# Bias tiles read from 128 stored copies of each bias row instead of squares turned by matrix products, in a two-block kernel on one core

## The chip, the cores and the metric

The kernel runs on one core of a Trainium2 chip. The metric is the time of one execution on the device in microseconds (us), taken as the median of several runs. All arithmetic is in float32; the large matrix products split every operand into a high and a low part and add three products of the fp32r type.

## What is computed

Two transformer blocks follow each other, each of two layers, on 256 tokens of width 1024. The first has a mixer, cross attention to a memory and a gated feed-forward part in each layer; the second has a feed-forward part, a mixer of three attentions and another feed-forward part. What the change touches is the bias that two of the three attentions of the second block add to their scores: a table of 32 buckets by 12 heads, looked up by the distance from query to key.

```
def t5_bucket(dist):
    max_exact = NUM_BUCKETS // 2
    d = jnp.maximum(dist, 0)
...
s_w = (jnp.einsum('bgrqd,bgkd->bgrqk', qb, kb).astype(jnp.float32) * scale
       + head_bias[:, :, t5_bucket(dist_w)])
...
s = (jnp.einsum('bgrqd,bgkd->bgrqk', qb, kb).astype(jnp.float32) * scale
     + head_bias[:, :, t5_bucket(dist)])
```

The bias of one head depends on the distance alone, so a row of 383 numbers holds all that 128 queries and 256 keys need; the tile of 128 by 256 that a score product takes has that row shifted by one element from each query to the next.

## The kernel before, in words

All operations go through a recorder (class `Pace`, whose wrapper is line 151), so every instruction of the trace stands under L151 and has to be told apart by the names of its tiles. The recorder also keeps a rough clock of its own while the program is written. Small pieces of work (attention heads, bias tables) are generators in a list `sides`; `pump` (line 343) writes the next step of a generator between two matrix products when the rough clock says that its inputs are there, and `finish` (line 373) forces out what is left of one. That clock thus sets the order in which instructions stand on each engine. On the chip each engine goes through its instructions in that order.

Weights come in 1 MB loads on SP's queue into three buffers `raw`, are split into `whi` on ScalarE (ACT) and `wlo` on VectorE (DVE), and are multiplied on TensorE (PE) into `acc`.

The function `cross` (line 1251) is the cross attention. It first makes the four blocks of queries (`stat_block`, products `acc` with a moving operand of 256 columns). Each head is then a side generator: products `aux<-mk,cqT` (scores), the row maximum `ngm` on DVE, exponentials `cpr` on ACT, division on DVE, transposes `aux<-ident,cpr` on PE, copy `cpt` on ACT, products `o<-cpt,mv`. After the last block come `finish(bias)` and `out_rows`, the output projection (products `acc` with 512 columns).

The bias of the second block is prepared in the two cross attentions of the first, as one more side generator:

- In layer 0, `bias_rows` (line 1358). Two small products `aux<-c,rb` make 12 rows of 383 (`u`, 12 partitions) and 8 rows of 480 (`uc`). SP stores `u` to `ud` in memory and `uc` to `ucd`, then loads from `ucd` two tiles `uk` with a shift of one element per partition; DVE adds `cmask` to columns of each `uk` (15 operations `bc`), and the result goes to `bcmp`. There is one buffer `uk`.
- In layer 1, `bias_squares` (line 1389). For each pair of heads SP loads `hk` from `ud`, with partition p starting at element p; these rows are in the reverse order. PE multiplies with `anti`, an identity with its columns reversed, ACT copies the product to `bts`, and SP stores that to `btiles`, two squares of 128 by 256 at a time. There are six pairs.

In the mixer of the second block `load_bias` (line 1470) loads one square per head from `btiles` on ACT's queue, 20 in each layer, into four buffers `bt`.

Of the kernel before, what the change touches and what calls it, by code (L numbers as in the profile page):

```python
# [8 lines left out]
F32 = mybir.dt.float32  # L9
# [9 lines left out]
DEPTH, D, S, P = 2, 1024, 256, 128  # L19
# [253 lines left out]
def tile_two_blocks(ctx, tc, I, out):  # L273
# [5 lines left out]
    def nm(s):  # L279
        count[0] += 1  # L280
        return f"{s}_{count[0]}"
# [20 lines left out]
    def aux():  # L302
        t = ps_aux.tile([P, 512], F32, tag="aux", name=nm("aux"))
        auxs.append(t.tensor.name)
        return t
# [20 lines left out]
    def mm(ps, a, b, start, stop, beside=False):  # L326

        nc.beside = beside
        nc.tensor.matmul(ps, a, b, start=start, stop=stop)
        nc.beside = False  # L330
# [4 lines left out]
    def side(gen):  # L335
        sides.append([gen, nc.end, False])
# [36 lines left out]
    def finish(gen):  # L373
        while any(i[0] is gen for i in sides):
            pump(force=True)
# [271 lines left out]
    def const(pool, name, dt=F32, tag=None):  # L647
        lo_, hi_ = C128[name]
        t = pool.tile([P, hi_ - lo_], F32, tag=f"c_{name}", name=nm(name), bufs=1)
        nc.sync.dma_start(t, cst[:, lo_:hi_])  # L650
        return t
# [599 lines left out]
    def cross(l, norm, next_maker):  # L1251
        T = norm.T
        with nc.pool(tc, name=nm("cross"), bufs=2) as mp:

            def load_kv(h):
                out_ = []
                for kind in ("k", "v"):
                    t = mp.tile([P, 2, S], F32, tag=f"m{kind}", name=nm(f"m{kind}"))
                    nc.scalar.dma_start(t.rearrange("p b n -> p (b n)"), kvd[l, kind][h])
                    out_.append(t)  # L1260
                return out_

            kv = {h: load_kv(h) for h in (0, 1)}
            heads = {}
            bias = (bias_rows, bias_squares)[l](mp)
            side(bias)
            O = split_T()

            def head(h, qT):
                yield True  # L1270
                kT, v = kv.pop(h)
                ps = aux()
                for t in (0, 1):
                    for c in (0, 1):
                        mm(ps[:, t * S : (t + 1) * S], qT[:, c, t * P : (t + 1) * P], kT[:, c, :], start=c == 0, stop=c == 1)
                ngm, sums = sm(2, "ngm"), sm(2, "csum")
                nc.vector.tensor_reduce(ngm, ps.rearrange("p (t k) -> p t k", t=2), axis=AX.X, op=ALU.max, negate=True)
                for t in (0, 1):
                    nc.vector.tensor_scalar(ngm[:, t : t + 1], ngm[:, t : t + 1], norm.r[t], None, op0=ALU.mult)
                pr = mp.tile([P, 2, S], F32, tag="cpr", name=nm("cpr"))  # L1280
                for t in (0, 1):
                    nc.scalar.activation(pr[:, t, :], ps[:, t * S : (t + 1) * S], AF.Exp, bias=ngm[:, t : t + 1], scale=norm.r[t], accum_out=sums[:, t : t + 1])
                ri = sm(2, "cri")
                nc.vector.reciprocal(ri, sums)
                for t in (0, 1):
                    nc.vector.tensor_scalar(pr[:, t, :], pr[:, t, :], ri[:, t : t + 1], None, op0=ALU.mult)
                yield True
                ps = aux()
                for t in (0, 1):
                    for c in (0, 1):  # L1290
                        turn(ps[:, c * S + t * P : c * S + (t + 1) * P], pr[:, t, c * P : (c + 1) * P], ident)
                pt = mp.tile([P, 2, S], F32, tag="cpt", name=nm("cpt"))
                nc.scalar.copy(pt.rearrange("p c q -> p (c q)"), ps)
                yield True
                ob = obank(f"o{h % 2}")
                yield from until(nc.free[ob.tensor.name])
                for d in (0, 1):
                    for c in (0, 1):
                        mm(ob[:, d * S : (d + 1) * S], v[:, c, d * P : (d + 1) * P], pt[:, c, :], start=c == 0, stop=c == 1)
                ov = ob.rearrange("p (d q) -> p d q", d=2)  # L1300
                put(O.hi[:, 2 * h : 2 * h + 2, :], O.lo[:, 2 * h : 2 * h + 2, :], ov)
                for kt in (2 * h, 2 * h + 1):
                    O.ready.add((kt, 0))
                    O.ready.add((kt, 1))
                if h < 2:
                    kv[h + 2] = load_kv(h + 2)

            def q_done(h):
                def f(a):
                    if h >= 2:  # L1310
                        finish(heads[h - 2])
                    qT = mp.tile([P, 2, S], F32, tag="cqT", name=nm("cqT"))
                    nc.scalar.activation(qT.rearrange("p c q -> p (c q)"), a[:, :512], AF.Copy, scale=1.0 / 16)
                    heads[h] = head(h, qT)
                    side(heads[h])
                return f

            for h in range(4):
                stat_block(T, 2, 2, q_done(h))
            chain = next_maker()  # L1320
            finish(bias)
            out_rows(lambda k: (O, 0), 8, 4 if units["ffn", l] else 5, chain, units["ffn", l])
        return chain.next

# [25 lines left out]
            nc.scalar.activation(dst.rearrange("p t f -> p (t f)"), a, AF.Sin)  # L1350


    btiles = dpool.tile([12, P, S], F32, tag="btiles", name="btiles")
    bcmp = dpool.tile([P, 240], F32, tag="bcmp", name="bcmp")
    ud = dpool.tile([12, 384], F32, tag="ud", name="ud")
    ucd = dpool.tile([8, 480], F32, tag="ucd", name="ucd")

    def bias_rows(bp):

        one = lambda shape, tag: bp.tile(shape, F32, tag=tag, name=nm(tag), bufs=1)  # L1360
        c32, rb, um, u = one([32, 863], "c32"), one([32, 12], "rb"), one([12, 383], "um"), one([12, 384], "u")
        for t, s_ in ((c32, c32d), (rb, I["rel_bias_2"]), (um, I["umask"])):
            nc.sync.dma_start(t, s_)
        cmask = const(bp, "cmask")
        nc.gpsimd.memset(u[:, 383:], 0.0)
        yield nc.products + 12.0
        ps = aux()
        mm(ps[:12, :383], rb, c32[:, :383], start=True, stop=True)
        nc.vector.tensor_tensor(u[:, :383], ps[:12, :383], um, op=ALU.add)
        nc.sync.dma_start(ud, u)  # L1370
        yield
        ps = aux()
        mm(ps[:8, :480], rb[:, :8], c32[:, 383:863], start=True, stop=True)
        uc = one([8, 480], "uc")
        nc.vector.tensor_copy(uc, ps[:8, :480])
        nc.sync.dma_start(ucd, uc)
        bc = one([P, 2, 4, 2, 15], "bc")
        for t in (0, 1):

            hk = one([P, 8, 225], "uk")  # L1380
            nc.sync.dma_start(hk, bass.AP(tensor=ucd.tensor, offset=ucd.offset + t * P, ap=[[1, P], [480, 8], [1, 225]]))
            yield True
            for n in range(15):
                k = 224 - 16 * n
                nc.vector.tensor_tensor(bc[:, t, :, :, n], hk[:, :, k].rearrange("p (g r) -> p r g", g=2),
                                        cmask[:, t * 15 + n : t * 15 + n + 1].unsqueeze(1).to_broadcast([P, 4, 2]), op=ALU.add)
        nc.sync.dma_start(bcmp, bc.rearrange("p t r g n -> p (t r g n)"))

    def bias_squares(bp):

        anti = const(bp, "anti")
        hks = []

        def load(h):
            hk = bp.tile([P, 2, S], F32, tag="hk", name=nm("hk"))
            nc.sync.dma_start(hk, bass.AP(tensor=ud.tensor, offset=ud.offset + h * 384, ap=[[1, P], [384, 2], [1, S]]))
            hks.append(hk)

        load(0)
        for h in range(0, 12, 2):  # L1400
            if h + 2 < 12:
                load(h + 2)
            yield nc.products + (12.0 if h == 0 else 2.5)
            ps = aux()
            mm(ps, anti, hks.pop(0).rearrange("p h k -> p (h k)"), start=True, stop=True)
            bt = bp.tile([P, 2, S], F32, tag="bts", name=nm("bts"))
            nc.scalar.copy(bt.rearrange("p h k -> p (h k)"), ps)
            nc.sync.dma_start(btiles[h : h + 2].rearrange("h p k -> p h k"), bt)

    def plan_mixer2(l):  # L1410
        w = I["w_in_2"][l]
# [20 lines left out]
    def mixer2(l, T, next_maker):  # L1432
        with nc.pool(tc, name=nm("mix2"), bufs=2) as mp:
# [35 lines left out]

            def load_bias(h):  # L1470
                t = mp.tile([P, S], F32, tag="bt", name=nm("bt"), bufs=4)
                nc.scalar.dma_start(t, btiles[h])
                return t

            def probs(ring, ps, bias, sum_, ngm, first=1e38):
# [598 lines left out]
```

## Time and profile before

| | us |
|---|---|
| median of 3 runs | 2095.59 |
| lowest and highest run | 2090.49, 2095.66 |
| the profiled execution | 2099.48 |
| its span, first to last instruction | 2097.7 |
| PE busy | 2040.0 (97%) |
| DVE busy | 1251.1 (60%) |
| ACT busy | 1096.9 (52%) |

The profiled execution is 3.9 us longer than the median of the runs; 1.8 us of it lie outside its span. Busy time of PE contains time in which its products overlap or run at a lower granted clock. Times in the trace are us from the start of the span.

### The profile page before, as it was taken

The numbers are of one execution on the slowest core, as the hardware profiler recorded it, in microseconds if no ns is written. First come the engines' busy times: TensorE is split into PE (matmuls) and PEld (weight loads), VectorE is DVE, ScalarE is ACT, GpSimd is POOL, SyncE is SP. The second block draws the span as 40 slices with busy tenths as digits, with TensorE's granted clock in tenths as the row PEclk, the third lists the DMA queues.
The fourth block names the chain that finished last, engine by engine and source line by source line (L and its number), as shares of the span: only waits on it lengthen the run. The fifth ranks groups of instructions, "written<-read, shape, count | busy, mean of one in ns | idle before, by whom it ended". The sixth has DMA issues, their size and how long they took to land.

```text
span 2097.7 us, 27293 instructions
## 1 busy us (share of the span) xinstructions
PE 2040.0 (97%) x10446; PEld 1673.8 (80%) x10446; DVE 1251.1 (60%) x2123; ACT 1096.9 (52%) x1842; POOL 92.7 (4%) x112
## 2 busy tenths in 40 slices
PE   7999999999999999999999999999999998999999
PEld 6788888888787788788887677888888886778887
DVE  6766565556763655556466566664565564666553
ACT  5556565445564654555454545654554463546542
POOL 0210000001200000000000000000000000000000
PEclk9999999999999999999999999999999999999999
DMA  7555565645465555465545644555555455555552
GB/s 241 184 191 190 184 203 179 220 160 189 166 212 157 194 183 207 162 201 176 198 142 172 215 135 165 193 180 200 181 181 193 164 186 171 170 151 184 178 199 102
DMA packets 200610, 380.79 MB, mean 182 GB/s; under 512 B 14288, under 2 KB 70400, under 8 KB 200480
## 3 DMA queue, kind: packets, MB, share of 16 engines
q1 hardware_dynamic: 188960, 366.46, 53.0%
q10 hardware_dynamic: 11520, 12.59, 2.0%
q8 instruction: 82, 1.34, 0.2%
q14 instruction: 48, 0.39, 0.1%
HBM read 372.03 MB, written 6.99 MB: 181 GB/s over the span
## 4 chain that ended last, share of the span: by engine, by line
PE 82%; DVE 7%; ACT 4%; DMA 4%; issue 2%; POOL 1%; SPq 0%; ACTq 0%; DVEq 0%; POOLq 0%
PE acc L151 74%; PE aux L151 7%; DVE wlo L151 3%; DMA raw<-in_w_in_dram 2%; PE o L151 2%; ACT whi L151 2%; DMA hk<-ud 1%; ACT thi L151 1%; DVE h L151 0%; ACT cpr L151 0%; DVE rs L151 0%; DVE t L151 0%; DMA mem<-in_mem_dram 0%; DVE ngm L151 0%; DMA nb<-cdram 0%
## 5 line engine op out<-in xcount | busy, mean ns | idle before, releaser
L151 PE MATMUL acc<-whi,thi 128*128 128x512 f32 (+1 forms) x1760 | 704.2, 400 | 6.8 <-ACT kvout L151 2.7
L151 PE MATMUL acc<-whi,tlo 128*128 128x512 f32 (+1 forms) x1760 | 685.0, 389 | 2.7 <-DVE tlo L151 2.6
L151 PE MATMUL acc<-wlo,thi 128*128 128x512 f32 (+1 forms) x1760 | 684.0, 389 | 2.8 <-DVE wlo L151 2.6
L151 DVE TENSOR_TENSOR wlo<-raw,whi 128x1024 fp32r<-128x1024 f32 (+1 forms) x370 | 443.2, 1212 | 293.9 <-ACT whi L151 292.7
L151 ACT CAST whi<-raw 128x1024 fp32r<-128x1024 f32 (+1 forms) x370 | 377.1, 1037 | 259.0 <-PE acc L151 209.3
L151 DVE SCALAR_TENSOR_TENSOR wlo<-raw,prm,whi 128x512 fp32r<-128x512 f32 (+1 forms) x592 | 392.4, 718 | 177.2 <-ACT whi L151 176.9
L151 ACT ACTIVATE whi<-raw,prm 128x512 fp32r<-128x512 f32 (+1 forms) x592 | 371.6, 694 | 93.2 <-PE acc L151 89.7
L151 PEld LDWEIGHTS acc<-whi,thi 128*128 128x128 f32 x1760 | 332.8, 189 | 85.1 <-issue 14.2
L151 PEld LDWEIGHTS acc<-whi,tlo 128*128 128x128 f32 x1760 | 332.1, 189 | 74.9 <-DVE tlo L151 6.7
L151 PEld LDWEIGHTS acc<-wlo,thi 128*128 128x128 f32 x1760 | 333.0, 189 | 66.6 <-DVE wlo L151 6.0
L151 PE MATMUL acc<-whi,ahi 128*128 128x512 f32 x528 | 206.8, 392 | 0.3
L151 PE MATMUL acc<-whi,alo 128*128 128x512 f32 x528 | 205.6, 389 | 0.0
L151 PE MATMUL acc<-wlo,ahi 128*128 128x512 f32 x528 | 205.5, 389 | 0.0
L151 POOL TENSOR_TENSOR r<-v,mhalf 128x1 f32<-128x1 f32 (+3 forms) x46 | 52.2, 1135 | 1538.4 <-DVE v L151 1538.4
L151 DVE SCALAR_TENSOR_TENSOR silu<-acc,r,silu 128x512 f32<-128x512 f32 (+1 forms) x72 | 47.5, 702 | 118.2 <-PE acc L151 94.2
L151 PEld LDWEIGHTS acc<-whi,ahi 128*128 128x128 f32 x528 | 99.1, 188 | 21.6 <-ACT whi L151 1.5
L151 PEld LDWEIGHTS acc<-whi,alo 128*128 128x128 f32 x528 | 99.1, 188 | 20.7
L151 PEld LDWEIGHTS acc<-wlo,ahi 128*128 128x128 f32 x528 | 99.2, 188 | 20.0
L151 PE MATMUL acc<-thi,whi 128*128 128x256 f32 x384 | 113.0, 294 | 0.0
L151 ACT ACTIVATE silu<-acc,r 128x512 f32<-128x512 f32 (+1 forms) x72 | 43.1, 650 | 127.7 <-PE acc L151 127.6
L151 PE MATMUL acc<-tlo,whi 128*128 128x256 f32 x384 | 108.6, 283 | 0.0
L151 PE MATMUL acc<-thi,wlo 128*128 128x256 f32 x384 | 108.5, 283 | 0.0
(299 smaller groups left out, 1815.7 us busy)
## 6 DMA issues: line engine op xcount, KB each, us to landing
raw<-in_w_in_dram SPq DMA_DIRECT2D x65, 1024.0 KB, 5.1
raw<-in_ffn_w_down_dram SPq DMA_DIRECT2D x44, 1024.0 KB, 4.9
raw<-in_ffn_w_gate_dram SPq DMA_DIRECT2D x40, 1024.0 KB, 5.0
raw<-in_ffn_w_up_dram SPq DMA_DIRECT2D x40, 1024.0 KB, 5.0
raw<-in_w_down_dram SPq DMA_DIRECT2D x22, 1024.0 KB, 4.8
raw<-in_w_gate_dram SPq DMA_DIRECT2D x20, 1024.0 KB, 5.0
raw<-in_w_up_dram SPq DMA_DIRECT2D x20, 1024.0 KB, 5.0
raw<-in_w_out_dram SPq DMA_DIRECT2D x16, 1024.0 KB, 5.5
```

The lines of the kernel that those rows point to most:

```text
L151: return f(*args, **kwargs)
```

## The change

The store of 18 KB to `ud` becomes a store of the same 12 rows, each 128 times one after the other, to `urep`: 1536 rows of 384 floats, 2.36 MB. The source is still `u` on 12 partitions, with a step of 0 over the copies. `load_bias` takes a tile from the copies of its head: partition p starts at element 127 + 383 p, so each partition reads 256 floats one element earlier in the row than the one before, which is the order that the reversed identity gave. `bias_squares` is gone, with its six loads, products, copies and stores, its load of `anti` and the memory `btiles`; the cross attention of layer 1 has no bias work.

```
-            bias = (bias_rows, bias_squares)[l](mp)
-            side(bias)
+            bias = bias_rows(mp) if l == 0 else None
+            if bias:
+                side(bias)
...
-            finish(bias)
+            if bias:
+                finish(bias)
             out_rows(lambda k: (O, 0), 8, 4 if units["ffn", l] else 5, chain, units["ffn", l])
...
-    btiles = dpool.tile([12, P, S], F32, tag="btiles", name="btiles")
+    urep = dpool.tile([12, P, 384], F32, tag="urep", name="urep")
...
-        nc.sync.dma_start(ud, u)
+        nc.sync.dma_start(urep, u.unsqueeze(1).to_broadcast([12, P, 384]))
...
-    def bias_squares(bp):
-
-        anti = const(bp, "anti")
...
-            yield nc.products + (12.0 if h == 0 else 2.5)
-            ps = aux()
-            mm(ps, anti, hks.pop(0).rearrange("p h k -> p (h k)"), start=True, stop=True)
-            bt = bp.tile([P, 2, S], F32, tag="bts", name=nm("bts"))
-            nc.scalar.copy(bt.rearrange("p h k -> p (h k)"), ps)
-            nc.sync.dma_start(btiles[h : h + 2].rearrange("h p k -> p h k"), bt)
...
-                nc.scalar.dma_start(t, btiles[h])
+
+                nc.scalar.dma_start(t, bass.AP(tensor=urep.tensor, offset=urep.offset + h * P * 384 + P - 1, ap=[[383, P], [1, S]]))
```

The change also moves instructions, since the recorder's clock counts the bytes of the new store. In the cross attention of layer 0, DVE has these rows around the first operations on `uk`, before the change:

```order
L151 TENSOR_TENSOR wlo_2288<-raw_1987,whi_2287 128x1024
L151 TENSOR_TENSOR bc_2230<-uk_2231,cmask_2068 128x8 x15
L151 TENSOR_TENSOR tlo_1951<-o_2335,thi_1950 128x512
L151 TENSOR_TENSOR wlo_2349<-raw_2087,whi_2348 128x1024
L151 TENSOR_REDUCE ngm_2363<-aux_2358 128x2
```

and with it:

```order
L151 TENSOR_TENSOR wlo_2287<-raw_1986,whi_2286 128x1024
L151 TENSOR_TENSOR tlo_1950<-o_2317,thi_1949 128x512
L151 TENSOR_TENSOR wlo_2331<-raw_2086,whi_2330 128x1024
L151 TENSOR_TENSOR bc_2229<-uk_2230,cmask_2067 128x8 x15
L151 TENSOR_REDUCE ngm_2362<-aux_2357 128x2
```

The 15 additions to the first `uk` now stand straight ahead of the row maximum `ngm` of the last head. On PE, at the same place, the last head's scores are followed before the change by 12 products of the output projection (the first three of them are shown), its transposes, 6 more products and `o`:

```order
L151 MATMUL acc_2245<-tlo_1590,whi_2077 128x256
L151 MATMUL acc_2245<-thi_1589,wlo_2078 128x256
L151 MATMUL aux_2358<-mk_2221,cqT_2352 128x256 x4
L151 MATMUL acc_2391<-whi_2120,thi_1950 128x512
L151 MATMUL acc_2391<-wlo_2121,thi_1950 128x512
L151 MATMUL acc_2391<-whi_2120,tlo_1951 128x512
```

and with it by nothing in between:

```order
L151 MATMUL acc_2244<-thi_1588,wlo_2077 128x256
L151 MATMUL aux_2357<-mk_2220,cqT_2334 128x256 x4
L151 MATMUL aux_2374<-ident_90,cpr_2367 128x128 x4
L151 MATMUL o_2381<-cpt_2379,mv_2222 128x256 x4
L151 MATMUL acc_2404<-whi_2119,thi_1949 128x512
L151 MATMUL acc_2404<-wlo_2120,thi_1949 128x512
```

`finish(bias)` now drives the last head to its end ahead of the output projection, and those 18 products come after `o`. On SP the row `urep<-u` stands where `ud<-u` stood, ahead of `ucd<-uc` and `uk<-ucd`. In the cross attention of layer 1, SP has before the change, from the third and fourth load of output weights on:

```order
L151 DMA raw_5908<-in_w_co_dram 128x2x1024
L151 DMA btiles<-bts_5937 128x2x256
L151 DMA hk_5940<-ud 128x2x256
L151 DMA btiles<-bts_5965 128x2x256
L151 DMA hk_5968<-ud 128x2x256
L151 DMA btiles<-bts_6004 128x2x256
L151 DMA hk_6007<-ud 128x2x256
L151 DMA raw_6025<-in_w_gate_dram 128x4x512
```

and with it:

```order
L151 DMA raw_5805<-in_w_co_dram 128x2x1024
L151 DMA raw_5901<-in_w_co_dram 128x2x1024
L151 DMA raw_5997<-in_w_gate_dram 128x4x512
L151 DMA gain_6043<-in_post_cross_g_dram 128x1024
L151 DMA raw_6082<-in_w_gate_dram 128x4x512
```

All stores to `btiles` and loads of `hk` are gone between the weight loads, and on PE the six products with `hk` are gone while the order of the heads stays interleaved with other products.

## Rows read from the trace of the kernel before

**Rows 1.** The profile page: the chain that ended last, by line.
```profile
PE acc L151 74%; PE aux L151 7%; DVE wlo L151 3%; DMA raw<-in_w_in_dram 2%; PE o L151 2%; ACT whi L151 2%; DMA hk<-ud 1%; ACT thi L151 1%; DVE h L151 0%; ACT cpr L151 0%; DVE rs L151 0%; DVE t L151 0%; DMA mem<-in_mem_dram 0%; DVE ngm L151 0%; DMA nb<-cdram 0%
```
**Rows 2.** Stretches: length, busy PE, PEld, DVE, ACT, POOL; granted clock, DMA share, GB/s.
```profile
614.40:662.70 48.30, 43.81 (x237) 36.01 (x238) 18.25 (x37) 21.17 (x42) 0.00 (x0) 0.96 0.61 198
193.00:234.20 41.20, 39.09 (x229) 32.86 (x230) 21.56 (x69) 17.76 (x37) 0.00 (x0) 1.00 0.59 202
```
**Rows 3.** The chain in order of time, cross attention of layer 1: start, us, what.
```profile
630.75 0.87 PE aux L151 x2
...
645.23 6.16 DMA hk<-ud
```
**Rows 4.** Groups of PE, 614 to 662: busy, mean ns | idle before, releaser.
```profile
L151 PE MATMUL aux<-hk,anti 128*128 128x512 f32 x12 | 6.3, 607 | 3.8 <-DMA hk<-ud 3.8
```
**Rows 5.** Instructions of PE in order: start, us, what [idle before].
```profile
225.41 1.99 PE L151 MATMUL aux<-mk,cqT 128*128 128x256 f32 x8 [1.41 <-ACT cqT L151]
...
651.53 1.10 PE L151 MATMUL aux<-hk,anti 128*128 128x512 f32 x2 [2.59 <-DMA hk<-ud]
652.46 3.47 PE L151 MATMUL aux<-mk,cqT 128*128 128x256 f32 x8
```
**Rows 6.** Stretch after the second wait for hk, columns as in rows 2.
```profile
652.50:656.00 3.50, 3.50 (x10) 2.79 (x9) 0.03 (x1) 0.59 (x1) 0.00 (x0) 0.52 0.25 91
```
**Rows 7.** Groups of PE, 205 to 216, layer 0.
```profile
L151 PE MATMUL aux<-c,rb 32*12 32x383 f32 (+1 forms) x4 | 1.8, 524 | 0.0
```
**Rows 8.** Instructions of SP in order, cross attention of layer 0: start, us of issue.
```profile
209.46 0.37 SPq L151 DMA_DIRECT2D raw<-in_w_co_dram  x1
210.70 0.32 SPq L151 DMA_DIRECT2D ud<-u  x1
213.90 0.29 SPq L151 DMA_DIRECT2D ucd<-uc  x1
215.98 0.38 SPq L151 DMA_DIRECT2D uk<-ucd  x1
221.45 0.40 SPq L151 DMA_DIRECT2D raw<-in_w_ck_dram  x1
222.60 0.36 SPq L151 DMA_DIRECT2D uk<-ucd  x1
```
**Rows 9.** DMA queues (packets, MB, share) and issues (count, KB, median us to landing).
```profile
q1 hardware_dynamic: 188960, 366.46, 53.0%
...
mk<-kvd ACTq DMA_DIRECT2D x8, 256.0 KB, 4.1
...
uk<-ucd SPq DMA_DIRECT2D x2, 900.0 KB, 7.0
hk<-ud SPq DMA_DIRECT2D x6, 256.0 KB, 5.2
...
bcmp<-bc SPq DMA_DIRECT2D x1, 120.0 KB, 1.7
```
**Rows 10.** Instructions of DVE in order, layer 0.
```profile
221.34 1.24 DVE L151 TENSOR_TENSOR bc<-uk,cmask 128x8 f32<-128x8 f32 x15
...
224.89 1.23 DVE L151 TENSOR_TENSOR wlo<-raw,whi 128x1024 fp32r<-128x1024 f32 x1 [0.25 <-ACT whi L151]
227.44 0.69 DVE L151 TENSOR_REDUCE ngm<-aux 128x2 f32<-128x512 f32 x1 [1.32 <-PE aux L151]
```
**Rows 11.** The chain in order of time, last head of layer 0.
```profile
230.32 0.70 PE aux L151 x4
231.03 1.40 PE acc L151 x6
232.42 1.73 PE o L151 x8
```
**Rows 12.** Instructions of ACT in order, the same head.
```profile
231.12 0.59 ACT L151 COPY cpt<-aux 128x512 f32<-128x512 f32 x1 [0.50 <-PE aux L151]
```
**Rows 13.** Tile bt: idle time of DVE before operations on it (us, times).
```profile
  DMA bt<-btiles: 13.1, 5
```

More of the change, by code (lines that the diff above doesn't have):

```diff
@@ L1350, in rotary_tables @@
             nc.scalar.activation(dst.rearrange("p t f -> p (t f)"), a, AF.Sin)
-    btiles = dpool.tile([12, P, S], F32, tag="btiles", name="btiles")
+    urep = dpool.tile([12, P, 384], F32, tag="urep", name="urep")
     bcmp = dpool.tile([P, 240], F32, tag="bcmp", name="bcmp")
-    ud = dpool.tile([12, 384], F32, tag="ud", name="ud")
     ucd = dpool.tile([8, 480], F32, tag="ucd", name="ucd")
@@ L1387, in bias_rows @@
         nc.sync.dma_start(bcmp, bc.rearrange("p t r g n -> p (t r g n)"))
-    def bias_squares(bp):
-        anti = const(bp, "anti")
[L1392 to L1402, printed above, removed]
-            yield nc.products + (12.0 if h == 0 else 2.5)
-            ps = aux()
-            mm(ps, anti, hks.pop(0).rearrange("p h k -> p (h k)"), start=True, stop=True)
-            bt = bp.tile([P, 2, S], F32, tag="bts", name=nm("bts"))
-            nc.scalar.copy(bt.rearrange("p h k -> p (h k)"), ps)
-            nc.sync.dma_start(btiles[h : h + 2].rearrange("h p k -> p h k"), bt)
     def plan_mixer2(l):
```

## The prediction

> **What bounds the kernel now.** I read the chain that ended last first. By line it is products on PE almost throughout, and the only transfer of the bias work in it is `hk<-ud` with 1% [rows 1]. So the kernel is bound by TensorE's work and by the few places where PE waits; a change is worth what it takes off PE there. Next I read the two cross attentions as stretches, each from the first head's scores to the end of the last head's `o`. They hold the same products in the program's order (126 with 256 columns, 18 with 512, four heads), yet layer 1 takes 48.3 us and layer 0 takes 41.2 [rows 2]. The reader should see that the longer one has less work on DVE (18.3 us against 21.6) and a granted clock of 0.96: what makes it long are products and waits of PE. Which waits is shown by PE's own rows and the chain [rows 3 to 6]. Last I read SP, DVE and PE around the bias rows in layer 0 [rows 8 to 12], since the new store stands there.
>
> **The change, part by part.**
>
> *Layer 1 loses the squares.* Six products of `hk` with the reversed identity go; each takes 0.87 us of the chain [rows 3], 5.2 us together. PE waits for `hk` twice, 3.8 us in all, the second time 2.6 us [rows 4, 5]; a load of `hk` took over 6 us there, from issue to release [rows 3]. [...] Sum 10.8 us. The stretches give a check: layer 1 is 7.1 us longer [rows 2], and layer 0 has two things that layer 1 won't have, 1.8 us of small products `c,rb` [rows 7] and a wait of 1.4 us for the last head's `cqT` [rows 5], which six products of the output projection will cover in layer 1: 7.1 + 1.8 + 1.4 = 10.3. I take 10.5 us gained. The six copies on ACT, the loads and stores on SP and the load of `anti` were beside this work and cost nothing of their own; nothing replaces them, and a head's chain stays covered by other products in layer 1. The weight loads behind them on SP come earlier. What is late next there is PE itself.
>
> *Layer 0 loses its cover.* After the last head's scores, PE now has that head's transposes and `o`, and only then the 18 products of the output projection which hid the latency. Those are 3 x 1.40 = 4.2 us of work [rows 11] that now comes after. Between transposes and `o` 0.65 us are won back: the transposes start at 230.32 and `o` at 232.42, but its input `cpt` is there at 231.12 + 0.59 = 231.7, so 1.4 us is enough instead of 2.1 [rows 11, 12]. Cost without any further wait: 3.55 us, plus 1.8 us if the clock falls in the gap of over 4 us that opens between scores and transposes, as it did after 2.6 us of idle in layer 1.
>
> *The store grows from 18 KB to 2.36 MB.* This decides the case. `ucd<-uc` stands behind it on SP's queue, and SP cannot issue the first `uk` before `ucd` has landed. The additions `bc` on that `uk` now stand on DVE right ahead of the last head's `ngm`. So: store late, `ucd` late, `uk` late, DVE blocked, PE idle with no product ahead of the head. Let T be the time that the store's data take.
> - Rates: queue q1 moved 366.46 MB in 53.0% of 16 engines' span of 2097.7 us, 20.6 GB/s for an engine that is busy, 330 for 16 [rows 9]. The store of 120 KB from 128 partitions lands in 1.7 us [rows 9], 0.37 of them data by that rate, so a transfer has 1.33 us beside its data.
> - Start: the weight load ahead is issued at 209.46 [rows 8] and has 1 MB, so its data end at 209.46 + 1.33 + 3.2 = 214.0. The store runs from 214.0 to 214.0 + T.
> - `ucd` lands some 0.7 us later, and `uk` is issued. The row of `uk` says 7.0 us [rows 9], of which a 1 MB load issued just ahead of the second one [rows 8] has 3.2; by rate it is 1.33 + 2.8 = 4.1. I take 4. `uk` is there at 218.7 + T.
> - DVE is free for it at 224.89 + 1.23 = 226.1 [rows 10], so T up to 7.4 us is hidden. Beyond that `bc` takes 1.24 us and `ngm` starts at 219.94 + T, against 227.44 before [rows 10]: T - 7.5 us late.
>
> With the lost cover the cost is T - 7.5 + 3.55 = T - 3.95 us, plus 1.8 for the clock.
>
> How long is T? No row has a large store from few partitions. Low end: all 16 engines at full rate, 2.36 MB / 330 = 7.2 us; if each of the 12 source rows has one engine, 9.6 us. High end: the rate goes with the share of 128 partitions, 12/128 of 330 = 31 GB/s, 76 us. The nearest row is `ucd`: 15 KB from 8 partitions were stored at 213.90 and released the next load at 215.98 [rows 8], 2.08 us, longer than the 1.7 us of the eight times larger store from 128 partitions [rows 9]. If the excess of 0.38 us is all data, 8 partitions give 40 GB/s and 12 give 61, T = 39 us; part of it may be the weight load still ahead, so this is rather too long. I take T = 27 us, the middle in ratio of 9.6 and 76, below the 39 of that row; the other values stay for the range.
>
> [...]
>
> *Reading the tiles.* 40 loads of 128 KB now start their partitions 1532 bytes apart, with 1 KB each as before. `hk` has such 1 KB runs one element apart: 5.2 us against 4.1 for 256 KB of `mk` [rows 9], so at most 0.55 us more for a `bt`, at least nothing. DVE waits five times for a `bt` [rows 13]: 0 to 2.8 us. The loads of `hk` stood between stores and weights, `mk` did not, so I take 0.
>
> *Sum.* -10.5 + (27 - 3.95) + 1.8 = +14.4 us: from the profiled 2099.5 to 2113.9. That execution was 3.9 us above the median of the runs, so for a median I add to 2095.6: **2110 us**. Break even lies at T = 12.7 us.
>
> **The rivals.**
> 1. *The store is quick and mostly covered (not slower).* For it: 12 or 16 engines at the rate that q1 shows. Against it: `ucd`. T = 9.6 gives -10.5 + 5.65 + 1.8 = -3.0, 2092.5 us; T up to 7.4 gives -5.2, 2090.4, and 2088.6 if the clock stays up. It decides below T = 12.7. Between that and T = 19 the cost stays within 0.3% as well.
> 2. *The store takes longer than `ucd`'s rate says.* T = 39 gives 2122, T = 76 gives 2159. For it: partitions are few. Against it: most of `ucd`'s 2.08 us are common to all transfers.
> 3. *The bias tiles come later*, a new wait in the second block: +2.8 us on top, 2113. For it: the five waits; against: 1 KB runs stay 1 KB.
>
> **How the numbers follow.** About 0.3%, 6.3 us, is what a measurement of this kernel can tell from no change. Forecast (T from 19 to 39, rival 3 within it): 0.58. Rival 2 beyond T = 39: 0.09. T from 12.7 to 19: 0.09. Rival 1: 0.24, of which 0.06 for the gain of over 6.3 us that needs a hidden store and a steady clock. So slower 0.67, same 0.27, faster 0.06. The range reaches from the covered store, 2090, to T = 40, 2123; outside it are 0.05 below and 0.09 above. The forecast's own range is 2102 to 2122.
>
> **What would show it.** In layer 1, the stretch from the first scores to the last `o` near 38 us, no wait for `hk` and a clock of 1.00. In layer 0, `ucd` issued early but `uk` only some 28 us later, DVE idle before `bc<-uk`, PE idle for about 24 us before `ident,cpr`, and a low clock after it. The forecast is wrong if SP issues `uk` before about 230, or if PE's gap there is under 10 us; the step at fault is then T. If the gap is there and the time is not, the gain in layer 1 or the loads `bt` were mis-sized.

## The result and the profile after

The changed kernel takes **2117.78 us** (median of 5 runs, 2115.39 to 2119.97) against 2095.66 us for the kernel before in the same measurement: a ratio of 1.0107, 95% interval 1.0094 to 1.0119, so 22.1 us or 1.1% slower. The forecast was 2110 us in a range of 2090 to 2123. The profiled execution of the changed kernel took 2115.39 us, 2.4 us less than its median; the one before stood 3.9 us above its median. So the two traces differ by 15.9 us only, and what the change did is better read from stretches of them than from their ends.

The page's chain by line, the counterpart of [rows 1], has a new transfer in it, and `hk<-ud` is gone:

```profile
PE acc L151 75%; PE aux L151 7%; DVE wlo L151 3%; PE o L151 2%; DMA raw<-in_w_in_dram 2%; DMA ucd<-uc 1%; ACT whi L151 1%; ACT thi L151 0%; DVE h L151 0%; ACT cpr L151 0%; DVE t L151 0%; DVE ngm L151 0%; DVE x L151 0%; DMA uk<-ucd 0%; DVE tlo L151 0%
```

That 1% is the chain's wait for the little store behind the big one. Four views show how. The instructions of SP around the bias rows in layer 0 (start, us of issue), to be held against [rows 8]:

```profile
209.69 0.91 SPq L151 DMA_DIRECT2D urep<-u  x1
212.90 9.37 SPq L151 DMA_DIRECT2D ucd<-uc  x1
243.63 0.38 SPq L151 DMA_DIRECT2D uk<-ucd  x1
...
250.84 0.37 SPq L151 DMA_DIRECT2D uk<-ucd  x1
...
263.22 5.29 SPq L151 DMA_DIRECT2D raw<-in_w_gate_dram  x2
```

The first `uk` is issued at 243.63; before the change it was 215.98. Even to issue `ucd` took SP 9.37 us. DVE and PE at the same place (start, us, what, idle before), to be held against [rows 10 to 12]:

```profile
249.56 1.25 DVE L151 TENSOR_TENSOR bc<-uk,cmask 128x8 f32<-128x8 f32 x15 [24.45 <-DMA uk<-ucd]
250.72 0.69 DVE L151 TENSOR_REDUCE ngm<-aux 128x2 f32<-128x512 f32 x1
```

```profile
224.41 1.99 PE L151 MATMUL aux<-mk,cqT 128*128 128x256 f32 x8 [1.41 <-ACT cqT L151]
253.69 1.09 PE L151 MATMUL aux<-ident,cpr 128*128 128x128 f32 x4 [27.28 <-DVE cpr L151]
255.78 3.78 PE L151 MATMUL o<-cpt,mv 128*128 128x256 f32 x8 [1.01 <-ACT cpt L151]
```

DVE stands for 24.45 us in front of `bc`, with the last head's `ngm` behind it, and PE has no product to do for 27.28 us. The stretches, columns as in [rows 2], tell the rest:

```profile
642.85:698.03 55.18, 53.95 (x296) 45.89 (x297) 26.67 (x49) 25.55 (x51) 0.54 (x1) 1.00 0.43 150
642.80:682.50 39.70, 38.42 (x228) 33.18 (x229) 18.25 (x37) 17.74 (x36) 0.00 (x0) 1.00 0.45 159
191.99:284.79 92.80, 62.58 (x330) 52.36 (x331) 32.71 (x86) 29.01 (x57) 1.65 (x3) 0.83 0.58 148
...
230.20:260.90 30.70, 6.21 (x16) 4.85 (x17) 3.65 (x23) 3.09 (x7) 0.00 (x0) 0.50 0.63 143
```

The second row answers to the 48.30 us of [rows 2]: the cross attention of layer 1 is 8.6 us shorter, at a granted clock of 1.00 instead of 0.96. The third is layer 0 from its first head's scores to the first transposes `aux<-ident,x` behind the output projection, and the first is layer 1 measured in the same way. The same two stretches before the change, layer 0 and then layer 1:

```profile
192.99:254.57 61.58, 59.47 (x331) 50.20 (x332) 32.62 (x86) 28.81 (x57) 1.65 (x3) 1.00 0.54 186
```
```profile
614.40:678.89 64.49, 60.00 (x308) 49.30 (x309) 26.67 (x49) 28.99 (x57) 0.54 (x1) 0.97 0.55 178
```

Layer 0 lost 92.80 - 61.58 = **31.2 us**. Layer 1, between the starts of the same two products, went from 64.47 to 55.17 us and gained **9.3 us**. The difference, 21.9 us, is what the medians show (22.1). From these two stretches the experiments below are read as well; wherever nothing in them was changed they come out the same to 0.4 us in all traces, while executions differ by some us elsewhere.

### The profile page after: what moved, and what is told of

Read it like the earlier page. It is cut to its first block, busy times and chain, and to the rows that moved or that the text cites. A ratio compares the mean times of both kernels' runs of the same rounds, so it can differ in the third digit from the quotient of the medians.

```text
span 2113.6 us, 27236 instructions
## 1 busy us (share of the span) xinstructions
PE 2034.5 (96%) x10434; PEld 1670.8 (79%) x10434; DVE 1251.4 (59%) x2123; ACT 1093.5 (52%) x1836; POOL 92.6 (4%) x112
## 4 chain that ended last, share of the span: by engine, by line
PE 84%; DVE 6%; DMA 4%; ACT 4%; issue 2%; POOL 0%; ACTq 0%; SPq 0%; DVEq 0%
PE acc L151 75%; PE aux L151 7%; DVE wlo L151 3%; PE o L151 2%; DMA raw<-in_w_in_dram 2%; DMA ucd<-uc 1%; ACT whi L151 1%; ACT thi L151 0%; DVE h L151 0%; ACT cpr L151 0%; DVE t L151 0%; DVE ngm L151 0%; DVE x L151 0%; DMA uk<-ucd 0%; DVE tlo L151 0%
```

## Experiments: what makes the store slow

The theory after the result: T, the time of the store's data, is about 30 us because its twelve source rows lie side by side on partitions 0 to 11, and T goes one for one into PE's gap. By the trace's packet records the store's 1536 packets ran from 212.8 to 243.1 us, T = 30.3 us, and one took 213 ns in the median; a packet of `ud`, of the same 1536 bytes, took 65 ns in the run with the small store in the old order (below). Three runs move the rows of `u` to other partitions. The small product that makes the rows gets more columns for it, and ahead of it GpSimd clears two tiles and SP makes one more small load; the rest stays as it is.

```
-        c32, rb, um, u = one([32, 863], "c32"), one([32, 12], "rb"), one([12, 383], "um"), one([12, 384], "u")
+        c32, rb, um, u = one([32, 863], "c32"), one([32, 12], "rb"), one([23, 383], "um"), one([23, 384], "u")
+        rbs = one([32, 23], "rbs")
+        nc.gpsimd.memset(rbs, 0.0)
+        nc.gpsimd.memset(um, 0.0)
-        for t, s_ in ((c32, c32d), (rb, I["rel_bias_2"]), (um, I["umask"])):
+        for t, s_ in ((c32, c32d), (rb, I["rel_bias_2"]), (rbs[:, ::2], I["rel_bias_2"]), (um[::2], I["umask"])):
...
-        mm(ps[:12, :383], rb, c32[:, :383], start=True, stop=True)
+        mm(ps[:23, :383], rbs, c32[:, :383], start=True, stop=True)
...
-        nc.sync.dma_start(urep, u.unsqueeze(1).to_broadcast([12, P, 384]))
+        nc.sync.dma_start(urep, u[::2].unsqueeze(1).to_broadcast([12, P, 384]))
```

**Rows at a distance of 2 partitions.**

> The 12 rows of u lie on partitions 0, 2, 4 to 22 instead of 0 to 11, and the same 1536 packets of 1536 bytes leave from there; the order on every engine is that of the changed kernel. Theory (the store is slow for where its source rows lie: packets from neighbouring partitions stand in each other's way, T = 30.3 us): with twice the distance T halves to about 15 us, uk is issued some 15 us earlier, and the kernel takes 2102 to 2104 us. [...] Rival A (T is set by the number of source rows or of DMA engines that serve them, 12 either way) and rival B (T is set by the writing side in memory): T stays at 30 us and the time at 2117 to 2118 us.

Measured: 2099.55 us, ratio 1.0025 (1.0014 to 1.0036). T = 14.9 us, `uk` issued at 227.67, both as the theory said; the time is 2.5 us below the 2102 to 2104 that it gave.

**Rows at a distance of 9** (the same edit with 100 partitions and `::9`).

> As the run before, with the rows of u on partitions 0, 9, 18 to 99. Theory: T falls further; a quarter of 30.3 is 7.6 us, but 128 packets of a row, one behind the other at the 65 ns that a packet of ud took in the kernel before, are 8.3 us, so T = 8 to 10 us. Then the loss in layer 0 is 31.2 - 21 = 10 us or less, some 5 to 8 us with a shorter clock loss, and the kernel takes 2092 to 2097 us, the time of the kernel before. Rivals A and B: T stays at 30 us, 2117 to 2118 us. A rival C, that the reordering by itself costs most of the loss: T falls, but the time stays above 2105 us.

Measured: 2095.58 us, ratio 1.0004 (0.9994 to 1.0014). T = 9.3 us, `uk` issued at 224.10.

**Rows at a distance of 8** (89 partitions and `::8`).

> As the run with the rows of u on partitions 0, 9 to 99, with a distance of 8 instead of 9: partitions 0, 8 to 88. It tells whether what counts is the distance of neighbouring rows or the group that a partition belongs to. [...] Rival L (only closely neighbouring partitions stand in each other's way): T is 9 to 10 us, the rate 300 GB/s, the time 2094 to 2097 us.

Measured: 2098.35 us, ratio 1.0023 (1.0009 to 1.0038). T = 14.9 us, `uk` issued at 227.70.

The view of all DMA traffic in a stretch inside the store shows the rate: the changed kernel from 228 to 242 us, then the distance of 2 (219 to 226) and of 9 (218 to 223), a fence each. With the distance of 9 a part belongs to another queue (q1 is SP's queue, q10 ACT's; packets, MB, share):

```profile
DMA packets 701, 1.08 MB, mean 77 GB/s; under 512 B 0, under 2 KB 701, under 8 KB 701
```
```profile
DMA packets 708, 1.09 MB, mean 155 GB/s; under 512 B 2, under 2 KB 705, under 8 KB 708
```
```profile
DMA packets 975, 1.51 MB, mean 302 GB/s; under 512 B 11, under 2 KB 921, under 8 KB 975
...
q1 hardware_dynamic: 910, 1.40, 73.9%
q10 hardware_dynamic: 65, 0.11, 5.8%
```

and for the distance of 8 the same view, 40 slices of 214 to 230 us:

```profile
GB/s 346 348 216 200 200 204 207 198 227 212 201 204 211 193 227 207 212 250 228 192 155 108 96 108 104 96 108 104 96 108 97 93 60 0 0 0 20 58 270 295
```

The store alone ran at 77, 154 (1.08 MB in 7 us) and 280 GB/s (1.40 MB in 5 us), and one of its packets took 213, 113 and 65 ns in the median; 65 ns is what a packet of `ud` took. The packets, the number of rows and the destination are the same: neither the count of source rows nor the writing side sets T here (rivals A and B fall). The distance of 8 settles what the partitions have to do with it. It is hardly nearer than 9, but the store runs at about 200 GB/s until 222 us and then at 104, and lasts as long as with a distance of 2. So closeness alone does not set T (rival L falls). The author reads the two rates as some rows sharing something that others have to themselves, with the last rows deciding T; what they share no run shows.

An estimate from the runs' own numbers fits that reading. With 9 the store's 280 GB/s are 23 for each of its twelve rows, and 1536 bytes in the 65 ns of a packet are 24 GB/s, so there a row's packets follow one another: 128 of them at 65 ns are 8.3 of the 9.3 us. Held against 24 GB/s, the 77 GB/s of the changed kernel are what three such rows move, the 154 of the distance of 2 what six move, and with 8 the 200 at first are eight and the 104 at the end four.

PE's gap follows T one for one. The rows of PE for the distance of 2, of 9 and of 8:

```profile
237.69 1.09 PE L151 MATMUL aux<-ident,cpr 128*128 128x128 f32 x4 [11.85 <-DVE cpr L151]
```
```profile
234.08 1.09 PE L151 MATMUL aux<-ident,cpr 128*128 128x128 f32 x4 [6.20 <-DVE cpr L151]
```
```profile
237.64 1.08 PE L151 MATMUL aux<-ident,cpr 128*128 128x128 f32 x4 [10.69 <-DVE cpr L151]
```

From T = 30.3 to 14.9 and to 9.3 us the gap falls by 15.4 and by another 5.7 us; T fell by 15.4 and by 5.6. (With 8, PE's scores ended 1.1 us later in that execution, so the gap is 1.1 us shorter.)

## Experiments: the order, the queue, the engine in between

**The order alone.** The small store in the order of the changed kernel, with the recorder's clock still counting the large one.

```
-        nc.sync.dma_start(urep, u.unsqueeze(1).to_broadcast([12, P, 384]))
+        nc.sync.dma_start(ud, u)
+        nc.loads += 12 * (P - 1) * 384 * 4 / 360e3
...
-                nc.scalar.dma_start(t, bass.AP(tensor=urep.tensor, offset=urep.offset + h * P * 384 + P - 1, ap=[[383, P], [1, S]]))
+                nc.scalar.dma_start(t, bass.AP(tensor=ud.tensor, offset=ud.offset + h * 384, ap=[[1, P], [1, S]]))
```

> The order of the changed kernel on every engine, but the store writes each row once (18 KB, as before the change), and the tiles bt are read from these rows with partitions 4 bytes apart; so the reversal of the rows is left out and the bias tiles are mirrored. Theory: without the big store only the lost cover is paid in layer 0, 3.55 us and perhaps up to 1.9 us for the clock, and layer 1 keeps its gain of 9 to 10 us: 2089 to 2092 us. Rival C (the reordering, with bc ahead of ngm on DVE, costs much by itself): a gap of more than 10 us before the last head's transposes stays, and the time is over 2100 us.

Measured: 2091.81 us, ratio 0.9982 (0.9972 to 0.9991). PE's gap there is 3 us, and after it `o` is slow:

```profile
229.99 0.63 PE L151 MATMUL aux<-ident,cpr 128*128 128x128 f32 x4 [3.01 <-DVE cpr L151]
231.63 3.57 PE L151 MATMUL o<-cpt,mv 128*128 128x256 f32 x8 [1.01 <-ACT cpt L151]
```

The stretch of layer 0 is 67.12 us, 5.5 more than before the change. The lost cover of 3.55 us and 1.7 us for the slower `o` (3.57 us against 1.89 in the next run; 3.78 in the changed kernel, in the stretch with a granted clock of 0.50) make up 5.3 of it. The order costs 5.5 us, the store on top of it 25.7 of the 31.2.

**The gain alone.** The same small store without the line `nc.loads +=`, so that layer 0 keeps its old order.

> The gain alone: layer 0 in the order of before with the small store, no squares in layer 1, no copies in memory at all; the tiles bt are read from the rows themselves with partitions 4 bytes apart, so the reversal is left out and the bias tiles are mirrored. Theory: the gain in layer 1 is 9 to 10 us, and the memory-to-memory transfer of the earlier run cost nothing: 2085 to 2087 us, the time of that run within 2 us. Rival D (that transfer did cost something, or loads at a distance are dearer than neighbouring ones): this run is 3 us or more below that one, 2080 to 2082 us. The run with the small store in the new order less this one is the price of the order alone, which theory puts at 3.5 to 5.5 us.

Measured: 2083.44 us, ratio 0.9952 (0.9935 to 0.9968); layer 0 61.55 us, as before the change, layer 1 55.16. The time is 1.6 us below the theory's 2085 and above rival D's 2082; beside the two runs with the copies below (0.9962 and 0.9947) no price of those copies can be told from the noise.

**The store on the other queue.**

```
-        nc.sync.dma_start(urep, u.unsqueeze(1).to_broadcast([12, P, 384]))
+        nc.scalar.dma_start(urep, u.unsqueeze(1).to_broadcast([12, P, 384]))
```

> The changed kernel with one thing moved: the big store of urep is issued on ACT's queue instead of SP's; rows on partitions 0 to 11 as in the changed kernel, order on all engines else the same. Theory (what costs the time is that ucd and uk stand behind the store on SP's queue): the store still takes 28 to 35 us, but uk is issued some microseconds after ucd, by 220 us instead of 243.6, and PE's gap ahead of the last head's transposes falls from 27.3 to 3 to 9 us: 2092 to 2098 us. [...]

Measured: 2111.74 us, ratio 1.0084 (1.0063 to 1.0106). The theory's numbers are wrong here: `uk` is issued at 230.28 instead of by 220 us, and the time lies 13.7 us above its range. SP, ACT, DVE and PE in order:

```profile
212.46 0.30 SPq L151 DMA_DIRECT2D ucd<-uc  x1
230.28 0.37 SPq L151 DMA_DIRECT2D uk<-ucd  x1
```
```profile
209.15 1.38 ACTq L151 DMA_DIRECT2D urep<-u  x1
...
210.60 8.98 ACTq L151 DMA_DIRECT2D mk<-kvd  x1
219.62 5.00 ACTq L151 DMA_DIRECT2D mv<-kvd  x1
```
```profile
246.80 1.25 DVE L151 TENSOR_TENSOR bc<-uk,cmask 128x8 f32<-128x8 f32 x15 [7.54 <-DMA uk<-ucd]
```
```profile
226.31 3.78 PE L151 MATMUL aux<-mk,cqT 128*128 128x256 f32 x8 [12.66 <-ACT cqT L151]
...
243.60 3.75 PE L151 MATMUL aux<-mk,cqT 128*128 128x256 f32 x8 [6.45 <-DMA mk<-kvd]
250.93 1.03 PE L151 MATMUL aux<-ident,cpr 128*128 128x128 f32 x4 [3.58 <-DVE cpr L151]
```

One gap became three, 22.7 us together. ACT itself is held for 14 us by the issues of `mk` and `mv` behind the store, so `cqT` is late; `mk` is late; and `ucd`, on a queue of its own behind a weight load that landed at 213.0, still took until 230 us. `uk` then took from 230.28 to the start of `bc` at 246.80, 16.5 us instead of 5.9 in the changed kernel. So it is not only SP's queue. What stands behind the store on its queue waits, and so do a small store and a load on the other one.

**The same with `uc` on other partitions**, to tell the side of the partitions from the DMA engines.

```
+        rb2 = one([32, 72], "rb2")
+        nc.gpsimd.memset(rb2, 0.0)
+        nc.gpsimd.tensor_copy(rb2[:, 64:72], rb[:, :8])
...
-        mm(ps[:8, :480], rb[:, :8], c32[:, 383:863], start=True, stop=True)
+        mm(ps[:72, :480], rb2, c32[:, 383:863], start=True, stop=True)
...
-        nc.sync.dma_start(ucd, uc)
+        nc.sync.dma_start(ucd, uc[64:72])
```

> The run with the big store on ACT's queue, with one more edit: the rows of uc lie on partitions 64 to 71 instead of 0 to 7, so the store of ucd (on SP's queue) no longer leaves from partitions that the big store reads; the product behind it has 72 columns of weights, and one small copy on GpSimd makes them. In the earlier run ucd was issued at 212.5 us and uk only at 230.3, though nothing stood ahead of ucd on SP but a weight load. Theory H (ucd waited at the partitions' side, where both stores read): uk is now issued within 4 us of ucd, at 215 to 218 us. Theory I (the DMA engines are busy with the big store's packets and a small store gets its turn late, wherever it reads): uk stays at 225 us or later. In both the loads mk and mv stand behind the big store on ACT's queue and are late, so PE keeps its gaps of 12 and 6 us there; the time stays near 2106 to 2112 us and is not what tells.

Measured: 2112.66 us (two runs), ratio 1.0085 (1.0066 to 1.0103), and SP as before:

```profile
212.74 0.30 SPq L151 DMA_DIRECT2D ucd<-uc  x1
230.15 0.38 SPq L151 DMA_DIRECT2D uk<-ucd  x1
```

Theory H falls, and theory I's sign came: `ucd` waits for its turn wherever it reads. That the turn is one on the DMA engines is not shown, since the records name no engine. The packet records show both effects apart. The first of the eight packets of `ucd` came 15.7 us after the issue (228.5 us), and 15.9 us in the run before, wherever they read; but one took 79 ns on partitions 64 to 71 and 289 ns beside the store's rows. In both runs 849 of the store's 1536 packets had ended by then; why the turn came at that point stays open.

**The additions off DVE.**

```
-                nc.vector.tensor_tensor(bc[:, t, :, :, n], hk[:, :, k].rearrange("p (g r) -> p r g", g=2),
+                nc.gpsimd.tensor_tensor(bc[:, t, :, :, n], hk[:, :, k].rearrange("p (g r) -> p r g", g=2),
```

> The changed kernel with the two groups of 15 additions bc moved from DVE to GpSimd, nothing else. The store, ucd and uk stay as late as they are (T = 30 us, uk issued at 243 to 244 us). Theory (the late uk reaches PE only over bc, which stands ahead of the last head's ngm on DVE): PE's gap falls from 27.3 to about 3 us, as in the run with the small store. What is late next are the weights behind uk on SP: the first w_gate would still be issued at 263 us or later instead of 239, so a new wait of PE of up to 10 us may open in the feed-forward part: 2090 to 2102 us. Rival G (the late transfers hold PE in another way, for instance over the weights w_ck issued behind uk, so the gap only moves): 2110 us or more.

Measured: 2100.68 us, ratio 1.0038 (1.0023 to 1.0053). T = 30.3 us and `uk` is issued at 244.00, as late as ever, but PE's gap is that of the small store:

```profile
229.18 2.86 PE L151 MATMUL aux<-mk,cqT 128*128 128x256 f32 x8 [3.41 <-DMA mk<-kvd]
235.04 1.09 PE L151 MATMUL aux<-ident,cpr 128*128 128x128 f32 x4 [3.01 <-DVE cpr L151]
...
271.27 0.80 PE L151 MATMUL acc<-whi,thi 128*128 128x512 f32 x1 [2.18 <-ACT thi L151]
```

So 24 us of the gap, 27.28 less 3.01, reach PE over `bc` on DVE. The rest is the late transfers again: `mk` landed at 229.04, 17.6 us after its issue in that execution (7.5 us in the trace of the changed kernel), and `w_gate`, issued at 260.7, came too late. The first load of it landed at 265.7; ACT's split of it began at 265.81 after 7.5 us of idle, with `thi` behind it on ACT, and PE waits for `thi` at 271.27; the stretch behind the output projection is 5.9 us longer. Here the theory's numbers hold, the late weights among them.

## Experiments: two versions that keep the gain

**Copies from memory to memory, in layer 1.** Layer 0 as before the change; one transfer from `ud` to `urep`.

```
+    urep = dpool.tile([P, 12 * 384], F32, tag="urep", name="urep")
...
+            else:
+                nc.sync.dma_start(urep, bass.AP(tensor=ud.tensor, offset=ud.offset, ap=[[0, P], [1, 12 * 384]]))
...
+                nc.scalar.dma_start(t, bass.AP(tensor=urep.tensor, offset=urep.offset + h * 384 + P - 1, ap=[[12 * 384 - 1, P], [1, S]]))
```

> Layer 0 as in the kernel before the change (rows stored once, 18 KB, in the order of before); at the start of layer 1's cross attention one transfer from memory to memory writes the 128 copies, 128 rows of 18 KB, each partition's copy one after the other; bt is read from there at a distance of 4607 elements. Theory: layer 0 loses nothing, layer 1 gains 9 to 10 us and the transfer delays only weight loads that are early enough: 2085 to 2087 us, below both kernels. Rival D (the transfer of 2.36 MB holds back the weight loads behind it on SP's queue and PE waits for them in layer 1): 2090 us or more, with a wait of PE or of the weight splits for raw after 614 us. If the gain in layer 1 was overrated, 2090 to 2095 us without such a wait.

Measured: 2085.66 us, ratio 0.9962 (0.9951 to 0.9974).

> The kernel with the copy from memory to memory in layer 1 once more, beside the run before this one on the same chip. It took 0.9962 of the kernel before; theory: 0.995 to 0.997 again, within 2 us of the run with the spread rows stored late, since both keep the gain of layer 1 of 9 to 10 us and should pay nothing in layer 0. Rival D as before: if the memory-to-memory transfer delays weights in layer 1, it is 3 us or more behind that run.

Measured: 2084.31 us, ratio 0.9947 (0.9935 to 0.9959). Layer 0 takes 61.58 us in both, layer 1 55.14 and 55.35 against 55.16 without the transfer: at most 0.2 us of waiting for it.

**Rows at a distance of 9, stored late.** The edit of the distance of 9, with the store moved behind `bcmp`, its bytes not counted by the recorder.

```
         nc.sync.dma_start(bcmp, bc.rearrange("p t r g n -> p (t r g n)"))
+        loads = nc.loads
+        nc.sync.dma_start(urep, u[::9].unsqueeze(1).to_broadcast([12, P, 384]))
+        nc.loads = loads
```

> The rows of u on partitions 0, 9 to 99; layer 0 in the order of before; the big store is issued behind bcmp, so that on SP's queue it has only weight loads of the feed-forward part behind it. Theory: T stays near 9 us, uk is issued as early as in the kernel before, PE has no new gap in layer 0, and the weight loads, up to 9 us later, are still early enough: 2083 to 2086 us, the gain of layer 1 in full. Rival J (the weights w_gate are then too late, as in the run with bc on GpSimd, where they came some 22 us later and cost PE 6 us): a wait of ACT for raw at 250 to 262 us and a time of 2087 to 2092 us.

Measured: 2084.10 us, ratio 0.9949 (0.9937 to 0.9961). Layer 0 takes 61.65 us. SP shows what stands behind the store now:

```profile
229.84 0.86 SPq L151 DMA_DIRECT2D urep<-u  x1
230.80 5.42 SPq L151 DMA_DIRECT2D raw<-in_w_gate_dram  x2
```

The two versions are equal within their intervals and 0.4 to 0.5% faster than the kernel before. That is the gain of layer 1 without the loss of layer 0.

All runs in one table. Loss and gain are the stretches of layer 0 and 1 less 61.58 and 64.47 us; their sum should be the change in time.

| run | T | loss | gain | sum | ratio, in us of 2095 |
|---|---|---|---|---|---|
| changed kernel | 30.3 | 31.2 | -9.3 | +21.9 | +22.4 |
| distance 2 | 14.9 | 15.9 | -9.3 | +6.6 | +5.2 |
| distance 8 | 14.9 | 15.6 | -9.3 | +6.3 | +4.8 |
| distance 9 | 9.3 | 9.5 | -9.3 | +0.2 | +0.8 |
| small store, new order | - | 5.5 | -9.3 | -3.8 | -3.8 |
| small store, old order | - | 0.0 | -9.3 | -9.3 | -10.1 |
| store on ACT's queue | 30.2 | 28.7 | -9.0 | +19.7 | +17.6 |
| and `uc` apart | 30.0 | 27.9 | -9.0 | +18.9 | +17.8 |
| `bc` on GpSimd | 30.3 | 11.2 + 5.9 | -9.3 | +7.8 | +8.0 |
| memory to memory | - | 0.0 | -9.3 | -9.3 | -8.0 |
| the same again | - | 0.0 | -9.1 | -9.1 | -11.1 |
| distance 9, late | 9.6 | 0.1 | -9.3 | -9.2 | -10.7 |

## Why the prediction was right, and where its terms were off

The sign, the mechanism and the range were right: the store behind which `ucd`, `uk`, DVE's `bc`, the last head and PE stand in a row outweighs the gain of layer 1. By its steps:

- *T, taken as 27 us.* Measured 30.3; this is the term that decided, and it was mis-sized by 3.3 us. Taken as the middle in ratio of two far ends, it lay near the truth by luck of those ends rather than by reading. The row of `ucd`, which gave 39, was nearer in kind (few partitions) but mixed its fixed part with its data. Which partitions the rows lie on is in none of these values, yet the same twelve rows and bytes took 14.9, 14.9 and 9.3 us at distances of 2, 8 and 9.
- *T goes one for one into PE's gap; the reordering costs 3.55 us.* Both right: the gap falls by 15.4 and 5.7 us for 15.4 and 5.6 of T, and the order alone costs 5.5, 1.7 of it the slower `o`. That DVE's `bc` is what passes the wait on was shown by moving it: the gap fell from 27.28 to 3.01 us.
- *`uk` in 4 us from issue to `bc`.* It took 249.56 - 243.63 = 5.9; 1.9 us too little. In the runs with distances of 2 and 9 it was 5.9 us as well, so this is not the store's doing: the estimate by the rate of the queue is 4.1, and the row of `uk`, 7.0, was discounted too far.
- *The clock, 1.8 us (also a term of layer 1's 10.8).* No run shows this value: the trace before has 1.5 us for a head's scores after the second wait for `hk` [rows 5, 6], and the rest was the author's estimate. In place of it, after 27.28 us without work PE ran at a granted clock of 0.50 until 260.9: 6.21 us of busy time by the row of that stretch, of which 3.1 us are lost, an estimate by that clock. In layer 1 only 3.5 us of products ran at the low level, 0.52 [rows 6].
- *Layer 0 together:* predicted 27 - 3.95 + 1.8 = 24.9, measured 31.2. T, `uk` and the clock are off by 3.3 + 1.9 + 1.3 = 6.5 us, which is the 6.3 us between the two to 0.2.
- *Layer 1, 10.5 us.* Measured 9.3. Waits for `hk` of 3.8 us are gone, but waits of PE for `cqT` rose from 0.2 to 0.6 us; the scores, part of them at a granted clock of 0.52 before [rows 6], gave 1.5 (9.4 us of products before, 7.9 after). The rest, 4.4 us, is put down to the six products, 0.73 each instead of 0.87; it is a remainder and was not measured apart. The stretch to the last `o` was to be 38 us and is 39.7.
- *Reading the tiles, taken as 0.* Right for the time: the wait of DVE rose by 0.4 us. But a load took longer than the 0.55 us allowed for, 4.1 us to landing in the median against 2.6 before (2.8 and 3.5 in the two runs at a distance of 9, with the same reads), so the loads became slower and stayed covered for the most part. The counterpart of [rows 13] in the trace after, with the landing:

```profile
  DMA bt<-urep: 13.5, 5
...
DMA to landing us min/median/max: 2.0/4.1/7.3
```

and the landing before:

```profile
DMA to landing us min/median/max: 2.0/2.6/7.5
```

The errors of layer 0 and layer 1 add up, 6.3 + 1.2 = 7.5 us, close to the 7.8 us between 2110 and 2117.8. Of the rivals, the quick store and the one of over 39 us fell with T, and the tiles that come later did not cost time. That a store of T = 9.3 us from the same place makes the change neutral is what the first rival said (2092.5 us; measured 2095.6).

## What to carry to other kernels

Before a large transfer is put on a queue, ask two things: on which partitions its source lies; and which small transfers come behind it whose results are needed by an instruction with others behind it on its engine, as `ngm` stood behind `bc` through 24.45 us of idle on DVE. Here the same 2.36 MB took T = 9.3 or 30.3 us by the choice of partitions, and the store of 9 us cost 9.5 us or 0.1 by its place in the program and the order that goes with it. A late store from partitions 0 to 11 was not run, so it is open whether the place alone would have been enough. A part of a change that gains (here, layer 1) should be measured without the part that pays for it; two versions then kept all of it.

## What was unexpected of the hardware

- A second queue did not help: `ucd`, 15 KB on a queue with no other load in flight from about 213 us on, began 15.7 us after its issue while the large store ran on the other queue, although the store moved some 77 GB/s only. The load `uk` behind it took 16.5 us instead of 5.9.
- A DMA issue held its engine: the issue of `ucd` behind the store took 9.37 us on SP (2.58 with the distance of 2, 1.46 with 9, 0.29 before the change), and those of `mk` and `mv` behind it 8.98 and 5.00 us on ACT, with 13.56 us of idle ahead of its next split `whi`.
